# A convolution block of a hybrid decoder: gates for all tokens first, then the values, with one set of weights at a time

## The chip, the cores and the metric

The kernel runs on one core of a Trainium2 chip. The metric is the device time of one execution in microseconds (us), lower is better; a time is the median of the runs shown. A difference of under 0.5% is about what a measurement of this kernel cannot tell from no change.

Engines are named as the profile names them: PE is TensorE (matrix products; PEld is its loading of weights), DVE is VectorE, ACT is ScalarE, POOL is GpSimd, SP is SyncE, which here only issues transfers (DMA). Each engine takes its instructions in order; between engines they wait for each other by semaphores.

## The reference

One layer of a decoder over 2048 prompt tokens and 32 sample tokens (8 sequences of 4). The input is normalised and multiplied by one wide matrix `w_in`, whose columns feed three branches (windowed attention, a gated causal convolution, cross-attention to a memory), their gates, and the merge. What matters here is the second branch:

```
h = _rmsnorm(x, g_pre) @ w_in
qa, ka, va, za, ub, zb, qc, zc, gt = jnp.split(h, SPLITS, axis=-1)
...
glu = ub[..., :EB] * jax.nn.sigmoid(ub[..., EB:])
...
full = jnp.concatenate([hist_conv, glu], axis=1)
conv = lax.conv_general_dilated(full, conv_w[:, None, :], window_strides=(1,), padding='VALID', ...,
                                feature_group_count=EB) + conv_b
```

`EB` is 768, so `ub` has 768 value columns and 768 gate columns; the convolution is 31 wide, one filter per channel.

## The kernel before, in words

The program has three stages, one after the other on PE: projections (`phase_a1`, up to about 898 us of the profiled execution), then the cross-attention, sample attention and windowed attention, with more projections as filler, then the merge and output (`phase_c`). The change lies in the first stage alone.

**Products in three passes.** All products keep float32 precision by splitting each factor into a high part `hi` and a remainder `lo`. `gemm` (line 156) multiplies eight blocks of 128 input channels; for each block it issues `hi` weights by high input (line 162), `hi` weights by low input (163), and `lo` weights by high input (164). The normalised input, as high and low parts for all 2080 tokens, lies in SBUF (tiles `x0h`, `x0l`, `x1h` and so on, the digit being the third of the tokens). Tokens go in six pieces, `CHUNKS`: four of 384, one of 256, one of 288.

**Weights.** `load_w` (141) brings 128 columns of a weight matrix in by a DMA on SP's queue (tile `wraw`, pool `wr`, two buffers), and POOL splits them: `whi` (line 55), then `wlo` (line 56), in the pool `w1` with two buffers each. So at most two sets of weights exist at a time; a third can be split only when PE has finished with the oldest.

**Order of the work.** `phase_a1` first computes two blocks of `q`, then goes through the list `order`: a convolution block `u0`, three plain blocks `k0`, `k1`, `k2`, then `u1`, `k3`, `k4`, `k5`, then `u2`, `v0` to `v2`, `u3`, `v3` to `v5`, `u4`, `q2` to `q4`, `u5`, `q5`, `qc0` to `qc3`. A plain block (`blk_x`, `chunk`) takes one set of weights for six chunks; ACT moves each result out of PSUM (line 233), and for `k` and `v` PE transposes it (250, 252) and DVE copies the rows (254, 258).

**A convolution block** (`blk_u`, 262) takes two sets of weights at once, `wb` for the gates and `wa` for the values. For each chunk it computes the gate product, ACT makes `th = tanh` of it (285), it computes the value product, and DVE writes (th + 1) x value into `G` (290; the sample tokens into `GS`, 295). Before that it clears the margins of `G` on POOL (268; `G` has two buffers) and brings in the old state of the sample sequences (`st_in`, 271, transposed at 275, copied at 277). Results of the products go through PSUM tiles `g`, four buffers.

**The convolution itself** (`conv`) runs on DVE alone: 60 instructions over `acc` and `G` (305, 314) and small ones for the sample tokens (317, 320), then the new state: `so` (325 to 327), three transposes on PE (`trc`, 330, 332), copies to `sr` (334, 335), and transfers on SP (`d_c` at 322, `conv_p` and `conv_s` at 337 and 338). It is issued with a lower priority (`later(LAG)`), so its instructions are spread under the blocks that follow.

**What sets the order on each engine** is a scheduler in the framework: it simulates the program with its own costs and priorities and writes one fixed order per engine. Instructions whose data come late in its simulation are put behind others.

Of the kernel before, what the change touches and what calls it, by code (L numbers as in the profile page):

```python
# [7 lines left out]
F32 = mybir.dt.float32  # L8
R32 = mybir.dt.float32r
AF = mybir.ActivationFunctionType  # L10
# [8 lines left out]
T = S + NS  # L19
HA, DA, EA = 12, 64, 768  # L20
EB, CW = 768, 31
# [9 lines left out]
CHUNKS = [(0, 384), (384, 384), (768, 384), (1152, 384), (1536, 256), (1792, 288)]  # L31
# [3 lines left out]
CQ, CK, CV, CZA, CUB, CZB, CQC, CZC, CGT = 0, 768, 1536, 2304, 3072, 4608, 5376, 5888, 6400  # L35


class K:
# [222 lines left out]

    def blk_u(self, j, wp, stg, cnv, psg, pst):
        nc, I, O = self.nc, self.I, self.O
        wb = self.load_w(wp, self.win(CUB + EB + j * 128), 8, rp=self.wr)
        wa = self.load_w(wp, self.win(CUB + j * 128), 8, rp=self.wr)
        G = cnv.tile([128, 16, 130], F32, name="G", bufs=2)
        GS = cnv.tile([128, 8, 34], F32, name="GS", bufs=2)
        nc.gpsimd.memset(G[:, :, 0:2], 0.0)

        st_in = cnv.tile([120, 2, 128], F32, name="st_in")  # L270
        nc.sync.dma_start(st_in, I["state_conv"][0, :, :, j * 128:(j + 1) * 128]
                          .rearrange("(x b) w c -> x (b w) c", x=2).rearrange("x q c -> q x c"))
        p = pst.tile([128, 512], F32, name="tr")
        for x in range(2):
            nc.tensor.transpose(p[:, x * 128:x * 128 + 120], st_in[:, x, :], self.ident[:120, :120])
        for x in range(2):
            nc.vector.tensor_scalar(GS[:, 4 * x:4 * x + 4, 0:30],
                                    p[:, x * 128:x * 128 + 120].rearrange("p (b w) -> p b w", b=4),
                                    2.0, None, op0=ALU.mult)
        for s, n in CHUNKS:  # L280
            xs = [self.x_at(k, s, n) for k in range(8)]
            pb = psg.tile([128, 512], F32, name="g")
            self.gemm(pb[:, :n], wb, xs)
            th = stg.tile([128, 384], F32, name="th")
            nc.scalar.activation(th[:, :n], pb[:, :n], AF.Tanh, scale=0.5)
            pa = psg.tile([128, 512], F32, name="g")
            self.gemm(pa[:, :n], wa, xs)
            m = min(n, S - s)
            r0 = s // 128
            nc.vector.scalar_tensor_tensor(G[:, r0:r0 + m // 128, 2:130],  # L290
                                           th[:, :m].rearrange("p (r i) -> p r i", i=128), 1.0,
                                           pa[:, :m].rearrange("p (r i) -> p r i", i=128),
                                           op0=ALU.add, op1=ALU.mult)
            if m < n:
                nc.vector.scalar_tensor_tensor(GS[:, :, 30:34],
                                               th[:, m:n].rearrange("p (b t) -> p b t", t=4), 1.0,
                                               pa[:, m:n].rearrange("p (b t) -> p b t", t=4),
                                               op0=ALU.add, op1=ALU.mult)
        return G, GS
# [995 lines left out]
```

## Time and profile before

| | |
|---|---|
| median of 3 runs | 3205.38 us (3191.82 to 3209.69) |
| profiled execution | 3205.15 us, span 3203.4 us |
| PE busy | 3017.2 us, 94% of the span |
| DVE, POOL, ACT busy | 2041.4, 1349.0, 1123.3 us |
| mean granted TensorE clock | 0.974 |

The span runs from the first to the last instruction; 1.75 us of the profiled execution lie around it. A row of a timeline gives the start, the duration, the engine, the line and the operation, the tile written and those read (`g<-x0h,whi`), the shape, and in brackets the idle time of that engine just before, with what ended it. PE's instructions overlap, so their spacing tells more than their durations.

### The profile page before, as it was taken

The page shows a single profiled execution, that of the slowest core. Times are in us where ns is not written, and L with a number is a line of the kernel's source. Part 1 is how long each engine was busy: PE and PEld are TensorE (multiplying, and loading weights), DVE is VectorE, ACT ScalarE, POOL GpSimd, SP SyncE. Part 2 cuts the span into 40 slices and gives each one's busy share as a digit, 9 for nine tenths or more (in the row PEclk, how much of TensorE's full clock was granted, in tenths as well). Part 3 has the DMA queues.
Part 4 walks back from the last instruction along what each step waited for, and adds up shares of the span by engine and source line. Part 5 has one row for each costly group of instructions (what it writes and reads, how often), then busy time and mean ns, then how long its engine had stood idle before and what let it go on. Part 6 is the DMA issues. An engine that isn't in the chain of part 4 may idle for free. (4 is left out here: it accounts for less than half of the span.)

```text
span 3203.4 us, 55580 instructions
## 1 busy us (share of the span) xinstructions
PE 3017.2 (94%) x20705; PEld 2856.5 (89%) x20705; DVE 2041.4 (64%) x3854; ACT 1123.3 (35%) x2835; POOL 1349.0 (42%) x1048
## 2 busy tenths in 40 slices
PE   7999999999988899999999999999898989999998
PEld 6899999999987889998899999999898967787897
DVE  5296786967967944555637666666657557555653
ACT  5110010000122433334437575766565623222221
POOL 0121222221336546444355576577667444233240
PEclk9899999999998999999999999999999999999999
DMA  6332221211254444378554655566655386757561
GB/s 223 107 99 74 80 58 53 57 62 63 73 170 129 158 138 151 109 224 252 157 139 106 159 131 151 129 171 176 161 140 153 104 273 214 228 171 222 158 201 54
DMA packets 532219, 454.67 MB, mean 142 GB/s; under 512 B 118191, under 2 KB 458581, under 8 KB 531137
## 3 DMA queue, kind: packets, MB, share of 16 engines
q1 hardware_dynamic: 357502, 335.36, 35.7%
q10 hardware_dynamic: 169840, 105.02, 11.5%
q0 software_dynamic: 4608, 10.75, 1.1%
q8 instruction: 164, 2.69, 0.4%
q14 instruction: 105, 0.86, 0.1%
HBM read 332.96 MB, written 118.04 MB: 141 GB/s over the span
## 5 line engine op out<-in xcount | busy, mean ns | idle before, releaser
L162 PE MATMUL gg<-x0h,whi 128*128 128x256 f32 (+1 forms) x2560 | 749.6, 293 | 35.5 <-DVE st L240 27.5
L164 PE MATMUL gg<-x0h,wlo 128*128 128x256 f32 (+1 forms) x2560 | 743.0, 290 | 3.3 <-POOL wlo L56 3.3
L163 PE MATMUL gg<-x0l,whi 128*128 128x256 f32 (+1 forms) x2560 | 744.1, 291 | 0.0
L55 POOL TENSOR_SCALAR whi<-wraw 128x1024 fp32r<-128x1024 f32 x162 | 203.1, 1255 | 952.2 <-PE g L163 547.8
L162 PEld LDWEIGHTS gg<-x0h,whi 128*128 128x128 f32 x2560 | 495.6, 194 | 43.3 <-DVE st L240 24.3
L164 PEld LDWEIGHTS gg<-x0h,wlo 128*128 128x128 f32 x2560 | 495.6, 194 | 6.0 <-POOL wlo L56 3.9
L163 PEld LDWEIGHTS gg<-x0l,whi 128*128 128x128 f32 x2560 | 495.6, 194 | 2.0 <-issue 0.3
L314 DVE SCALAR_TENSOR_TENSOR acc<-G,cw,acc 128x1536 f32<-128x1536 f32 (+15 forms) x354 | 460.5, 1334 | 0.0
L56 POOL TENSOR_TENSOR wlo<-wraw,whi 128x1024 fp32r<-128x1024 f32 x162 | 456.1, 2817 | 9.9 <-PE gg L164 0.6
L151 POOL TENSOR_TENSOR clo<-craw,chi 128x768 fp32r<-128x768 f32 (+1 forms) x96 | 172.0, 1793 | 357.2 <-ACT chi L150 344.8
L614 ACT ACTIVATE P<-T,stm 128x128 f32<-128x128 f32 (+1 forms) x576 | 260.7, 455 | 113.2 <-DVE stm L612 76.1
L162 PE MATMUL pg<-ac,chi 128*128 128x512 f32 (+1 forms) x640 | 229.6, 361 | 16.2 <-ACT chi L150 9.0
L612 DVE CUSTOM_DVE_ANT_0 T<-s,bias 128x128 f32<-128x128 f32 (+1 forms) x576 | 191.7, 357 | 77.7 <-PE s L604 43.2
L164 PE MATMUL pg<-ac,clo 128*128 128x512 f32 (+1 forms) x640 | 228.3, 358 | 5.7 <-POOL clo L151 5.5
L163 PE MATMUL pg<-ac,chi 128*128 128x512 f32 (+1 forms) x640 | 228.9, 358 | 2.8 <-DVE ac L1185 2.8
L233 ACT ACTIVATE st<-g 128x384 f32<-128x384 f32 (+1 forms) x132 | 60.2, 460 | 447.3 <-PE g L164 438.3
L164 PE MATMUL g<-x0h,wlo 128*128 128x384 f32 x544 | 187.1, 347 | 22.1 <-POOL wlo L56 22.1
L163 PE MATMUL g<-x0l,whi 128*128 128x384 f32 x544 | 189.5, 348 | 0.0
L162 PE MATMUL g<-x0h,whi 128*128 128x384 f32 x544 | 187.6, 346 | 0.0
L164 PE MATMUL g<-x1h,wlo 128*128 128x384 f32 x544 | 185.8, 341 | 0.0
L163 PE MATMUL g<-x1l,whi 128*128 128x384 f32 x544 | 185.0, 340 | 0.0
L162 PE MATMUL g<-x1h,whi 128*128 128x384 f32 x544 | 182.6, 339 | 2.3 <-ACT x1h L131 2.3
(329 smaller groups left out, 7477.5 us busy)
## 6 DMA issues: line engine op xcount, KB each, us to landing
wraw<-in_w_in ACTq DMA_DIRECT2D x119, 512.0 KB
d_g<-st ACTq DMA_DIRECT2D x168, 128.0 KB
cb<-d_cf SPq DMA_DIRECT2D x72, 256.0 KB
g<-d_g SPq DMA_DIRECT2D x72, 256.0 KB
wraw<-in_w_in SPq DMA_DIRECT2D x35, 512.0 KB
kvc<-in_cache_k_win SPq DMA_DIRECT2D x8, 1536.0 KB
kvc<-in_cache_v_win SPq DMA_DIRECT2D x8, 1536.0 KB
raw<-d_q SPq DMA_DIRECT2D x48, 256.0 KB
```

Source lines behind the costliest of these rows:

```text
L55: nc.gpsimd.tensor_scalar(hi, raw, 1.0, 1.0, op0=ALU.mult, op1=ALU.mult)
L56: nc.gpsimd.tensor_sub(lo, raw, hi.bitcast(F32))
L151: nc.gpsimd.tensor_sub(lo, raw, hi.bitcast(F32))
L162: nc.tensor.matmul(ps, hi[:, k, :], h, start=k == 0, stop=False)
L163: nc.tensor.matmul(ps, hi[:, k, :], l, start=False, stop=False)
L164: nc.tensor.matmul(ps, lo[:, k, :], h, start=False, stop=k == kb - 1)
L233: nc.scalar.activation(st[:, :n], p[:, :n], AF.Copy, scale=sc)
L314: nc.vector.scalar_tensor_tensor(a3[:, lo:hi], G[:, src:src + hi - lo, 2 - m:130 - m], w, a3[:, lo:hi], op0=ALU.mult, op1=ALU.add)
L612: nc.vector.tensor_tensor_reduce(sc[:, :w], t[:, o:o + w], bias[:, 256 - w:256], 1.0, 3.0e38, ALU.add, ALU.min, m)
L614: nc.scalar.activation(P[:, o:o + w], sc[:, :w], AF.Exp, bias=m, scale=-1.0, accum_out=self.stl[:, col:col + 1])
```

## The change

`blk_u` no longer interleaves gates and values. It loads the gate weights, computes all six chunks of gates, and ACT writes their tanh into a new tile `gate` of 2080 columns (one buffer; 8,320 bytes per partition). Then it loads the value weights into a further buffer of the same pools, computes all six chunks of values, and DVE forms `G` and `GS` from `gate` and the products. The tile `th` (three buffers of 384 columns, 4,608 bytes per partition in all) is gone. The clearing of `G` and the fetching of `st_in` now stand ahead of the weights in the code. Nothing else is touched; the number and the shapes of all instructions are the same.

```
     def blk_u(self, j, wp, stg, cnv, psg, pst):
         nc, I, O = self.nc, self.I, self.O
-        wb = self.load_w(wp, self.win(CUB + EB + j * 128), 8, rp=self.wr)
-        wa = self.load_w(wp, self.win(CUB + j * 128), 8, rp=self.wr)
         G = cnv.tile([128, 16, 130], F32, name="G", bufs=2)
...
+
+        w = self.load_w(wp, self.win(CUB + EB + j * 128), 8, rp=self.wr)
+        gate = cnv.tile([128, T], F32, name="gate")
         for s, n in CHUNKS:
-            xs = [self.x_at(k, s, n) for k in range(8)]
             pb = psg.tile([128, 512], F32, name="g")
-            self.gemm(pb[:, :n], wb, xs)
-            th = stg.tile([128, 384], F32, name="th")
-            nc.scalar.activation(th[:, :n], pb[:, :n], AF.Tanh, scale=0.5)
+            self.gemm(pb[:, :n], w, [self.x_at(k, s, n) for k in range(8)])
+            nc.scalar.activation(gate[:, s:s + n], pb[:, :n], AF.Tanh, scale=0.5)
+        w = self.load_w(wp, self.win(CUB + j * 128), 8, rp=self.wr)
+        for s, n in CHUNKS:
+            th = gate[:, s:s + n]
             pa = psg.tile([128, 512], F32, name="g")
-            self.gemm(pa[:, :n], wa, xs)
+            self.gemm(pa[:, :n], w, [self.x_at(k, s, n) for k in range(8)])
             m = min(n, S - s)
             r0 = s // 128
             nc.vector.scalar_tensor_tensor(G[:, r0:r0 + m // 128, 2:130],
```

**PE, block u1, from the end of its first gate chunk.** Before, with buffer numbers (`whi_2242` and `wlo_2243` are the gate weights, `whi_2248` and `wlo_2249` the value weights, `g_2289` the first value chunk, `g_2315` the second gate chunk):

```order
L162 MATMUL g_2289<-x0h0_186,whi_2248 128x384
L163 MATMUL g_2289<-x0l0_194,whi_2248 128x384
L162 MATMUL g_2315<-x0h0_186,whi_2242 128x384
L163 MATMUL g_2315<-x0l0_194,whi_2242 128x384
L164 MATMUL g_2315<-x0h0_186,wlo_2243 128x384
L162 MATMUL g_2315<-x0h1_187,whi_2242 128x384
L163 MATMUL g_2315<-x0l1_195,whi_2242 128x384
L164 MATMUL g_2315<-x0h1_187,wlo_2243 128x384
L162 MATMUL g_2315<-x0h2_188,whi_2242 128x384
L163 MATMUL g_2315<-x0l2_196,whi_2242 128x384
L164 MATMUL g_2315<-x0h2_188,wlo_2243 128x384
L164 MATMUL g_2289<-x0h0_186,wlo_2249 128x384
```

In the program after, at the same place (`whi_2247` and `wlo_2248` are the gate weights, `g_2278` the second gate chunk):

```order
L164 MATMUL g_2252<-x0h7_193,wlo_2248 128x384
L162 MATMUL g_2278<-x0h0_186,whi_2247 128x384
L163 MATMUL g_2278<-x0l0_194,whi_2247 128x384
L164 MATMUL g_2278<-x0h0_186,wlo_2248 128x384
L162 MATMUL g_2278<-x0h1_187,whi_2247 128x384
L163 MATMUL g_2278<-x0l1_195,whi_2247 128x384
L164 MATMUL g_2278<-x0h1_187,wlo_2248 128x384
```

Before, the first `wlo` product of the value weights stood some ten products behind the end of the first gate chunk, with as much of the second gate chunk as the scheduler put in between; now five more gate chunks stand ahead of any product with value weights.

**DVE, block u1, around the end of the convolution of u0** (`acc` is the running sum of that convolution, `G<-...` the products of u1). Before:

```order
L290 SCALAR_TENSOR_TENSOR G<-th,g 128x3x128
L314 SCALAR_TENSOR_TENSOR acc<-G,cw,acc 128x1536
L320 SCALAR_TENSOR_TENSOR acc<-GS,cw,acc 128x32
L314 SCALAR_TENSOR_TENSOR acc<-G,cw,acc 128x384
L314 SCALAR_TENSOR_TENSOR acc<-G,cw,acc 128x1664
L320 SCALAR_TENSOR_TENSOR acc<-GS,cw,acc 128x32
L314 SCALAR_TENSOR_TENSOR acc<-G,cw,acc 128x256
L290 SCALAR_TENSOR_TENSOR G<-th,g 128x3x128
L314 SCALAR_TENSOR_TENSOR acc<-G,cw,acc 128x1792
L320 SCALAR_TENSOR_TENSOR acc<-GS,cw,acc 128x32
L290 SCALAR_TENSOR_TENSOR G<-th,g 128x3x128 x2
L290 SCALAR_TENSOR_TENSOR G<-th,g 128x2x128 x2
```

After:

```order
L322 SCALAR_TENSOR_TENSOR acc<-GS,cw,acc 128x32
L316 SCALAR_TENSOR_TENSOR acc<-G,cw,acc 128x256
L316 SCALAR_TENSOR_TENSOR acc<-G,cw,acc 128x1792
L322 SCALAR_TENSOR_TENSOR acc<-GS,cw,acc 128x32
L292 SCALAR_TENSOR_TENSOR G<-gate,g 128x3x128 x4
L292 SCALAR_TENSOR_TENSOR G<-gate,g 128x2x128 x2
L297 SCALAR_TENSOR_TENSOR GS<-gate,g 128x8x4
L307 TENSOR_SCALAR acc<-G,cw,vecs 128x2048
```

The first two writes of `G` stood inside the tail of the previous convolution; now all six stand behind it, in one row. Line numbers after line 289 are two higher in the program after.

Three more places in words. On POOL the order is that of before: gate weights of u1, value weights of u1, the clearing of the `G` of u2, weights of `k3`. On SP the transfers `d_c` of a convolution and the raw weights keep their places; `conv_p` and `conv_s` stand three to six transfers later, in the middle of the next plain block. The three `trc` transposes on PE moved with them, from the end of u1 into the third chunk of `k3` (behind u2, u3 and u4 into the fourth or fifth chunk of the plain block or earlier, behind u5 into the second plain block), and the copies to `sr` on DVE, which wait for them, stand behind the first eleven or more `acc` instructions over `G` of the next convolution, where they stood ahead of all of them. From the second chunk of `qc0` on, PE's order is the same to the end of the program.

## Rows read from the trace of the kernel before

**Rows 1.** The page: the span, and PE's busy time, share and instructions.

```profile
span 3203.4 us, 55580 instructions
...
PE 3017.2 (94%) x20705; PEld 2856.5 (89%) x20705; DVE 2041.4 (64%) x3854; ACT 1123.3 (35%) x2835; POOL 1349.0 (42%) x1048
```

**Rows 2.** PE's waits from 0 to 1100 us: total, times, longest.

```profile
PE g L164 <- POOL wlo L56: 22.1, 4, 5.6
```

**Rows 3.** Timeline of PE in block u1.

```profile
242.82 0.69 PE L164 MATMUL g<-x0h,wlo 128*128 128x384 f32 x1 [5.58 <-POOL wlo L56]
...
246.02 0.33 PE L162 MATMUL g<-x0h,whi 128*128 128x384 f32 x1
```

**Rows 4.** Stretches: length, busy PE, PEld, DVE, ACT, POOL, granted clock, DMA, GB/s.

```profile
240.00:250.00 10.00, 7.18 (x33) 7.18 (x34) 9.09 (x13) 0.00 (x0) 2.77 (x1) 0.83 0.28 79
...
300.00:320.00 20.00, 20.00 (x135) 19.87 (x134) 20.00 (x23) 2.28 (x5) 4.28 (x2) 1.00 0.36 105
```

**Rows 5.** Timeline of POOL around block u1.

```profile
230.57 3.13 POOL L55 TENSOR_SCALAR whi<-wraw 128x1024 fp32r<-128x1024 f32 x1 [17.81 <-PE g L163]
233.78 8.98 POOL L56 TENSOR_TENSOR wlo<-wraw,whi 128x1024 fp32r<-128x1024 f32 x1
257.77 0.13 POOL L268 MEMSET G<- 128x32 f32 x1 [15.01 <-DVE acc L314]
...
281.93 2.40 POOL L56 TENSOR_TENSOR wlo<-wraw,whi 128x1024 fp32r<-128x1024 f32 x1
```

**Rows 6.** Timeline of ACT: the gates of blocks u1 to u5.

```profile
235.36 0.49 ACT L285 ACTIVATE th<-g 128x384 f32<-128x384 f32 x1 [4.25 <-PE g L164]
250.92 0.49 ACT L285 ACTIVATE th<-g 128x384 f32<-128x384 f32 x1 [15.07 <-PE g L164]
259.31 0.49 ACT L285 ACTIVATE th<-g 128x384 f32<-128x384 f32 x1 [7.89 <-PE g L164]
...
362.84 0.49 ACT L285 ACTIVATE th<-g 128x384 f32<-128x384 f32 x1 [4.25 <-DVE acc L314]
379.40 0.49 ACT L285 ACTIVATE th<-g 128x384 f32<-128x384 f32 x1 [16.07 <-PE g L164]
...
491.32 0.49 ACT L285 ACTIVATE th<-g 128x384 f32<-128x384 f32 x1 [4.25 <-PE g L164]
506.86 0.49 ACT L285 ACTIVATE th<-g 128x384 f32<-128x384 f32 x1 [15.04 <-PE g L164]
...
618.78 0.49 ACT L285 ACTIVATE th<-g 128x384 f32<-128x384 f32 x1 [4.24 <-PE g L164]
635.36 0.49 ACT L285 ACTIVATE th<-g 128x384 f32<-128x384 f32 x1 [16.10 <-PE g L164]
...
741.66 0.49 ACT L285 ACTIVATE th<-g 128x384 f32<-128x384 f32 x1 [3.70 <-PE g L164]
750.40 0.49 ACT L285 ACTIVATE th<-g 128x384 f32<-128x384 f32 x1 [8.26 <-PE g L164]
```

**Rows 7.** Timeline of DVE: the convolution of u0, from its start to its end.

```profile
157.47 1.88 DVE L305 TENSOR_SCALAR acc<-G,cw,vecs 128x2048 f32<-128x2048 f32 x1
...
175.73 2.48 DVE L314 SCALAR_TENSOR_TENSOR acc<-G,cw,acc 128x1280 f32<-128x1280 f32 x2
...
181.77 4.93 DVE L314 SCALAR_TENSOR_TENSOR acc<-G,cw,acc 128x1024 f32<-128x1024 f32 x2
...
255.16 0.56 DVE L290 SCALAR_TENSOR_TENSOR G<-th,g 128x384 f32<-128x384 f32 x1 [1.36 <-PE g L164]
...
257.63 0.25 DVE L320 SCALAR_TENSOR_TENSOR acc<-GS,cw,acc 128x32 f32<-128x32 f32 x1
```

**Rows 8.** PE's waits from 895 to 1000 us, behind the stage of the change.

```profile
PE sco L662 <- DVE sm L660: 9.0, 2, 5.8
PE gg L162 <- DVE st L240: 7.2, 3, 4.6
PE str L654 <- DVE sm L652: 4.7, 3, 1.6
```

## The prediction

> **What bounds the kernel now.** I read the page first: PE is busy for 3017.2 of 3203.4 us, 94% [rows 1]. So only what PE does or waits for counts, and the question is what PE loses in the stage that is changed, up to 898 us. The table of PE's waits answers that: behind the start-up, its one large entry there is a product with low weights that waits for POOL's split, 22.1 us in four waits, the longest 5.6 [rows 2]. The timeline shows where: in u1, PE stands still for 5.58 us ahead of the first product with the value weights' low part, and goes on slowly: that product takes 0.69 us, one of the same size 3.2 us later 0.33 [rows 3]. In that stretch of 10 us the mean granted clock is 0.83, where it is 1.00 in an undisturbed stretch in which PE is busy throughout [rows 4]. So a stall is paid twice, as idle time and as products at the lower of the two levels behind it.
>
> Why the value weights come late is seen on POOL. Two buffers exist; the gate weights of u1 have one, and the other is freed only when k2 ends. POOL starts the value split then, at 230.57, so PE leaves k2 at about 231, and finishes at 233.78 + 8.98 = 242.76 [rows 5]; PE goes on at 242.82 [rows 3]. PE needs these weights one gate chunk after the end of k2, some 4 us, and the split takes 12.2.
>
> **What the change removes.** I price all of it, idle time and slow products, on ACT, which runs the tanh of each gate chunk as soon as PE has it. Between two gate chunks lie one gate and one value chunk, 768 columns; undisturbed that takes 259.31 - 250.92 = 8.39 us. From the first to the second gate chunk of u1 to u5 it takes 15.56, 16.56, 15.54, 16.58 and 8.74 us [rows 6], 72.98 in all, so 72.98 - 5 x 8.39 = 31.0 us more than undisturbed. Of these, 22.1 are the waits, and 8.9 are slow products and small change; u5, which follows plain blocks without rows to copy, loses 0.35 only. u0 follows the start-up and has no such loss.
>
> **Where it goes.** In the new order the value weights are needed one whole set of gates later. Six chunks are 2080 columns, at 8.39 us for 768 columns 22.7 us. The buffer is freed where it was, so they are ready 12.2 us into 22.7, with 10.5 us to spare. So each half of a convolution block becomes what a plain block is today, and plain blocks, with the same two buffers, show no wait.
>
> The next set in line is that of k3. Its buffer is freed when the gates end, at about 231 + 22.7 = 253.7. But on POOL the clearing of the G of u2 stands ahead of it, and that waits for the end of u0's convolution: it ran at 257.77 [rows 5], just as DVE ended at 257.63 + 0.25 [rows 7]. So the split begins at 258 at the latest, takes 12.2 us at the worst seen, and ends by 270; PE needs it when the values end, at 231 + 45.4 = 276.4. The margin is 6 us at the worst. With DVE idle between its writes of G, the low split took 2.40 us instead of 8.98 [rows 5], which would add 6.6 us to the margin. The set behind it, of k4, starts when the values end and has a plain block's time, as today.
>
> **What it adds.** All six writes of G now come within 23 us, behind the tail of the previous convolution on DVE. That convolution ended at 257.9; the first value chunk ends at about 253.7 + 4.2 = 257.9. PE has four buffers for results, so the first must be free only three chunks later, 12.6 us. No cost, with 12.6 us of cover; if the tail came later than that, PE would wait for DVE microsecond for microsecond.
>
> The copies to `sr` now make DVE wait for three transposes on PE that stand in the third chunk of k3, behind 0.61 of its products. Behind them on DVE are the rest of the convolution and the copies of rows to come. DVE gets there after about what lies between 157.47 and 175.73 today [rows 7], 18 us; PE is there after 15, by columns 0.61 x 22.7 = 13.8 plus a few transposes. I take zero; the bound is a few us of DVE time, which the 12.6 us cover. On SP, the transfers of the new state stand behind stores of k3, and nothing reads them in the kernel.
>
> In u0 PE's first products stand in another order beside the bias products; the nearest row is u5's excess of 0.35 us [rows 6], so 0, give or take 1 or 2 us. The tile `gate` moves what the later stages find freed in SBUF; PE's waits there are 9.0, 7.2 and 4.7 us, 20.9 in all, for DVE [rows 8]. The orders there are the same, so I take 0; the bounds are that half of it goes, or that as much again comes, -10 to +21.
>
> **The sum.** 3205.15 us of the profiled execution - 31.0 = 3174.1. The median of the runs is 3205.38, 0.2 us away, so I leave it at 3174.
>
> **A rule against it.** The rows show first that POOL and DVE hinder each other: the low split took 8.98 us beside the convolution and 2.40 beside an idle DVE [rows 5], and in turn two convolution instructions beside another split took 4.93 us where larger ones took 2.48 [rows 7]. The Trainium skill, GPSIMD Engine Reference, "Key points", says why: GpSimd shares its SBUF interfaces with VectorE, and they contend where a DVE instruction has two SBUF inputs, as the convolution's have. By that rule a split put beside more of the convolution lengthens both, and the forecast could turn into the third rival below. The trace agrees on the mechanism, but the number of splits is the same and one of them now meets an almost idle DVE, so I give that rival a small chance.
>
> **The rivals.** First, the gain comes and a part is given back behind the stage. For it: the stage after is tangled, with waits in turn on DVE, ACT and transfers, and the tiles lie elsewhere. Against it: the orders are the same and the convolution of u5 hangs on PE's own progress. At half of the 20.9 us it gives 3174 + 10 = 3184, at all of it 3195.
>
> Second, the change does not do what it says: the wait only moves, from the first value chunk to the first chunk of k3, since POOL must now clear G before it splits for k3. It takes a convolution end more than 6 us later than today. Then each block loses some 5.5 us and its slow products again, and the time is 3205, no change. Against it: the convolution's tail now holds writes of G that wait for PE, 1.36 us for one of them [rows 7], and loses them.
>
> Third, slower than before: DVE's tail decides. If the contention lengthens a convolution so that it ends later than the 12.6 us of cover allow, PE waits for a buffer in each of five blocks (u1 to u5). Slower than before needs 31/5 = 6.2 us beyond the cover, an end 19 us later than today; at 10 us beyond it is 3174 + 5 x 10 = 3224, and with slow products of 2 us each 3234. At the 2.4 us or so that a split cost DVE in the row above, it would take eight more splits a block, and there are five.
>
> **How the numbers follow.** The forecast has a chance of 0.80, the gain partly given back 0.12, the wait that moves 0.05, DVE's tail 0.03. The range goes from 3160, the forecast less some 10 us of the later waits and a few us by which the median of a few runs moves (the runs shown lie from 3191.82 to 3209.69), to 3190, which takes in the first rival up to 16 us. A measurement of this kernel can tell about 0.5%, 16 us, from no change, so faster means under 3189.4: the forecast almost whole and most of the first rival, 0.89; the same 0.08, from the second and the rest; slower 0.03.
>
> **What would show it.** Right: no wait of PE for POOL's low split between 100 and 870 us, first to second gate chunk in u1 to u4 at about 4.2 us (one chunk now), a granted clock of 1.00 in these stretches, and the first product of the next stage some 31 us earlier. Wrong: a wait of PE at the first chunk of k3 behind POOL (second rival), a wait for DVE's writes of G (third), or larger waits in the 100 us after the stage (first).

## The result, and the profile after

The changed kernel takes 3169.14 us, median of the runs (3156.1 to 3174.24); the kernel before takes 3204.91 beside it. The ratio is 0.9888 [0.9869, 0.9906], 35.8 us less. The forecast was 3174, in the range 3160 to 3190. In a second comparison (e9 below) the ratio was 0.9899 [0.988, 0.9919].

The page of after, span and busy engines, as [rows 1]:

```profile
span 3154.0 us, 55551 instructions
...
PE 2992.8 (95%) x20705; PEld 2837.2 (90%) x20705; DVE 2037.6 (65%) x3854; ACT 1123.6 (36%) x2835; POOL 1368.9 (43%) x1048
```

The count of matrix products is the same, PE's busy time is 24.4 us less in this execution and 16.3 us less in that of e9. In the stage of the change, from the start to the mark `st<-gg` that is explained below, the same 5317 products keep PE busy for 851.51 us before and 838.67 after (838.22 in e9):

```profile
0.00:900.87 900.87, 851.51 (x5317) 835.16 (x5318) 644.61 (x838) 124.08 (x259) 198.49 (x80) 0.98 0.27 87
```

```profile
0.00:864.82 864.82, 838.67 (x5317) 825.51 (x5318) 642.36 (x838) 124.31 (x260) 216.06 (x80) 0.99 0.28 90
```

So of the 36.05 us by which this stage is shorter, 12.8 are products that went faster and 23.2 are idle time of PE that is gone.

The table of PE's waits has no row at all between 116 and 860 us, where [rows 2] had 22.1 us behind POOL. The stretch of 240 to 250 us of [rows 4] (length, busy time of PE, PEld, DVE, ACT and POOL, granted clock, DMA, GB/s) reads after:

```profile
240.00:250.00 10.00, 10.00 (x73) 10.00 (x71) 9.84 (x12) 1.29 (x3) 0.27 (x2) 1.00 0.24 68
```

PE is busy throughout and the granted clock stays at 1.00, the upper level, where [rows 4] had 7.18 us of 10 and 0.83.

ACT's timeline of after gives the marks of the stage, as [rows 6]: the first tanh of u0, the first two of u1, the first of u2, and ACT's first instruction on a result of the filler products behind the stage (`st<-gg`), which I use as the stage's end:

```profile
111.64 0.49 ACT L284 ACTIVATE gate<-g 128x384 f32<-128x384 f32 x1 [9.97 <-PE g L164]
...
230.69 0.49 ACT L284 ACTIVATE gate<-g 128x384 f32<-128x384 f32 x1 [4.25 <-DVE acc L316]
234.86 0.49 ACT L284 ACTIVATE gate<-g 128x384 f32<-128x384 f32 x1 [3.67 <-PE g L164]
...
350.90 0.49 ACT L284 ACTIVATE gate<-g 128x384 f32<-128x384 f32 x1 [4.26 <-DVE acc L316]
...
864.82 0.38 ACT L239 ACTIVATE st<-gg 128x256 f32<-128x256 f32 x1 [2.74 <-PE gg L164]
```

The same marks of before, as far as [rows 6] does not have them:

```profile
116.28 0.49 ACT L285 ACTIVATE th<-g 128x384 f32<-128x384 f32 x1 [14.82 <-PE g L164]
...
900.87 0.38 ACT L239 ACTIVATE st<-gg 128x256 f32<-128x256 f32 x1 [2.74 <-PE gg L164]
```

The stage ends 900.87 - 864.82 = 36.05 us earlier. From u1's first tanh to the end it is 665.51 us before and 634.13 after, 31.38 less: what the prediction summed up. The other 4.67 us are won ahead of u1 (235.36 against 230.69), and they are already there at u0's first tanh (116.28 against 111.64). The rest of the program took 3203.4 - 900.87 = 2302.5 us before and 3154.0 - 864.82 = 2289.2 in this execution, the shortest of its six; in e9 the stage ended at 865.14, the span was 3165.0, and the rest 2299.9. So those 13.3 us are mostly spread of the executions: PE is busy 11.6 us less there for the same products (2165.73 against 2154.11). The median's 35.8 us agree with the stage's 36.

POOL's timeline of after at the place of [rows 5]:

```profile
225.90 3.07 POOL L55 TENSOR_SCALAR whi<-wraw 128x1024 fp32r<-128x1024 f32 x1 [17.86 <-PE g L163]
229.05 9.05 POOL L56 TENSOR_TENSOR wlo<-wraw,whi 128x1024 fp32r<-128x1024 f32 x1
249.73 0.13 POOL L266 MEMSET G<- 128x32 f32 x1 [11.63 <-DVE acc L316]
249.84 1.05 POOL L55 TENSOR_SCALAR whi<-wraw 128x1024 fp32r<-128x1024 f32 x1
250.97 2.40 POOL L56 TENSOR_TENSOR wlo<-wraw,whi 128x1024 fp32r<-128x1024 f32 x1
272.05 1.05 POOL L55 TENSOR_SCALAR whi<-wraw 128x1024 fp32r<-128x1024 f32 x1 [18.67 <-PE g L163]
```

The split of the value weights is as slow as before (12.2 us) and ends at 238.10; PE's first value product comes at 249.13, 11 us later. The split for `k3` ends at 253.37, and PE leaves the values when it frees the buffer for the next split, at 272.05: 18.7 us to spare.

DVE's timeline at the end of u0's convolution, as the end of [rows 7]:

```profile
249.60 0.24 DVE L322 SCALAR_TENSOR_TENSOR acc<-GS,cw,acc 128x32 f32<-128x32 f32 x1
253.57 0.56 DVE L292 SCALAR_TENSOR_TENSOR G<-gate,g 128x384 f32<-128x384 f32 x1 [3.73 <-PE g L164]
```

The convolution ends 8 us earlier than before, 3.4 of them against u1's own start, which is 4.7 us earlier itself. DVE then waits for the value chunks, 3.73 us for the first, and not PE for DVE.

### The profile page after: what moved, and what is told of

It reads as the page before. It is cut to its first block, busy times and chain, and to the rows that moved or that the text cites. A ratio compares the mean times of both kernels' runs of the same rounds, so it can differ in the third digit from the quotient of the medians.

```text
span 3154.0 us, 55551 instructions
## 1 busy us (share of the span) xinstructions
PE 2992.8 (95%) x20705; PEld 2837.2 (90%) x20705; DVE 2037.6 (65%) x3854; ACT 1123.6 (36%) x2835; POOL 1368.9 (43%) x1048
## 3 DMA queue, kind: packets, MB, share of 16 engines
q10 hardware_dynamic: 169840, 105.02, 11.6%
q0 software_dynamic: 4608, 10.75, 1.1%
## 5 line engine op out<-in xcount | busy, mean ns | idle before, releaser
L55 POOL TENSOR_SCALAR whi<-wraw 128x1024 fp32r<-128x1024 f32 x162 | 221.4, 1368 | 918.0 <-PE g L163 534.7
```

What stands on the lines that cost most here:

```text
L55: nc.gpsimd.tensor_scalar(hi, raw, 1.0, 1.0, op0=ALU.mult, op1=ALU.mult)
```

## The experiments

Two questions stand. Is the wait for the second set of weights all that u1 to u5 had to lose (and what covers it now)? And what won 4.7 us in u0, which the prediction had at nothing? The theory for the second came from reading the two traces beside each other around u0's start, PE's timeline of before:

```profile
99.33 2.10 PE L354 MATMUL tr<-oh,rb 33*12 33x384 f32 x6
101.36 0.44 PE L162 MATMUL g<-x0h,whi 128*128 128x384 f32 x1
101.64 0.34 PE L163 MATMUL g<-x0l,whi 128*128 128x384 f32 x1
101.90 0.92 PE L364 MATMUL tr<-ohs,rb 33*12 33x376 f32 x2
102.75 0.69 PE L162 MATMUL g<-x0h,whi 128*128 128x384 f32 x1
...
104.97 3.93 PE L364 MATMUL tr<-ohs,rb 33*12 33x376 f32 x6
```

and of after:

```profile
99.36 2.10 PE L356 MATMUL tr<-oh,rb 33*12 33x384 f32 x6
101.39 0.44 PE L162 MATMUL g<-x0h,whi 128*128 128x384 f32 x1
...
103.00 2.06 PE L366 MATMUL tr<-ohs,rb 33*12 33x376 f32 x6
104.99 0.45 PE L164 MATMUL g<-x0h,wlo 128*128 128x384 f32 x1
105.27 0.34 PE L162 MATMUL g<-x0h,whi 128*128 128x384 f32 x1
```

The bias products (`bias_rows`: 33 rows of weights, 12 columns; a row of the trace counts each twice) lie between the token products of u0. Before, one `ohs` product came two token products behind the three `oh` ones, and from then on token products took longer, 0.69 us and then 0.52; after, eight token products lie between, and they go on at 0.34. The stretch 103 to 105 us, before and then after, with the granted clock in the third place from the end:

```profile
103.00:105.00 2.00, 2.00 (x7) 1.56 (x8) 0.39 (x1) 0.00 (x0) 2.00 (x2) 0.50 0.63 200
```

```profile
103.00:105.00 2.00, 2.00 (x8) 0.47 (x7) 1.07 (x2) 0.00 (x0) 2.00 (x2) 1.00 0.63 197
```

The clock is 0.50, the lower level, from 103 to 111 us before, and 1.00 after. Nothing in PE's waits shows it, for PE is busy all the time in both. The whole fall in the kernel before lies in this stretch:

```profile
102.00:113.00 11.00, 11.00 (x28) 6.63 (x28) 2.89 (x6) 0.00 (x0) 3.96 (x3) 0.53 0.53 165
```

With the clock at 0.53 in the mean, PE can do in these 11 us at most 5.2 us less work than at 1.00; that is an estimate, and it lies near the 4.7 us.

Marks in us from ACT's timeline: first tanh of u0 and u1, from u1's first tanh to u2's and to the first `st<-gg`, the time of that, and what is left of the profiled execution's span.

| | u0 | u1 | u1 to u2 | u1 to st<-gg | st<-gg | rest | ratio to before |
|---|---|---|---|---|---|---|---|
| before | 116.28 | 235.36 | 127.48 | 665.51 | 900.87 | 2302.5 | |
| after | 111.64 | 230.69 | 120.21 | 634.13 | 864.82 | 2289.2 | 0.9888 [0.9869, 0.9906] |
| e1, u0 old | 116.10 | 235.20 | 120.21 | 634.13 | 869.33 | 2300.8 | 0.9896 [0.9874, 0.9918] |
| e2, u0 alone new | 111.12 | 230.18 | 128.80 | 666.18 | 896.36 | 2299.4 | 0.9981 [0.9962, 0.9999] |
| e3, third set | 115.95 | 240.09 | 121.16 | 639.28 | 879.37 | 2279.4 | 0.9875 [0.9856, 0.9894] |
| e4, before, bias later | 108.17 | 235.20 | 127.45 | 665.44 | 900.64 | 2285.5 | 0.9944 [0.9924, 0.9964] |
| e5, after, bias later | 123.48 | 234.52 | 120.21 | 634.13 | 868.65 | 2277.8 | 0.9845 [0.9811, 0.988] |
| e6, split twice | 112.98 | 232.01 | 120.20 | 634.15 | 866.16 | 2309.0 | 0.9901 [0.9869, 0.9933] |
| e7, conv + 12 us | 113.10 | 232.15 | 120.22 | 634.42 | 866.57 | 2312.0 | 0.9897 [0.9859, 0.9935] |
| e8, conv + 30 us | 113.19 | 232.25 | 126.12 | 744.29 | 976.54 | 2301.3 | 1.0215 [1.0184, 1.0247] |
| e9, after again | 111.96 | 231.01 | 120.21 | 634.13 | 865.14 | 2299.9 | 0.9899 [0.988, 0.9919] |
| e10, e5 again | 125.01 | 234.86 | 120.20 | 634.13 | 868.99 | 2277.5 | 0.9859 [0.9841, 0.9878] |

In e5 and e10 ACT makes the first four tanh of u0 in one row, behind the last bias products; their mark of u0 can't be set beside the others, that of u1 can.

### e1 and e2: the change in u0 apart from u1 to u5

Both kernels have the two forms of the block, the old one with `th` as a slice of `gate`:

```
+    def blk_u_old(self, j, wp, stg, cnv, psg, pst):
...
-                        gs = self.blk_u(j, wp, stg, cnv, psg, pst)
+                        gs = (self.blk_u if j > 0 else self.blk_u_old)(j, wp, stg, cnv, psg, pst)
```

e2 has `j == 0` in that place.

> The changed kernel with one convolution block of six, u0, written in the old way (gates and values in turn, both sets of weights at once); u1 to u5 are as changed. PE's order around the bias products (tr<-oh, tr<-ohs) is again that of the kernel before, with one ohs product two token products behind the oh ones. Theory of the clock: the 4.7 us that the changed kernel won ahead of u1 hang on that order, so the granted clock falls to 0.50 again behind the ohs products, u1's first tanh comes at about 235.4 us (before 235.36, after 230.69) and the first filler result of stage one's end (st<-gg) at 900.9 - 31.4 = 869.5 us. Rival, chance: the fall in the kernel before was of that one execution and can be absent here; then about 230.7 and 864.8. Both expect the spacing u1 to u2 at 120.2 us, since it is the waits of u1 to u5 alone that the 31 us come from. Ratio to before 0.990 to 0.992 (clock) or 0.988 to 0.990 (chance).

> The other half: u0 alone is written in the new way, u1 to u5 are as before. The order around the bias products is that of the changed kernel. Theory of the clock: no fall of the clock at 100 to 113 us, u1's first tanh at about 230.7 us, the spacing u1 to u2 127.5 us as before, the four waits for wlo (22.1 us) back, the first st<-gg at 900.9 - 4.7 = 896.2 us, ratio 0.998 to 0.999. Rival, chance: the clock may fall here too, and u1's first tanh then comes at 235.4 us, st<-gg at 900.9. Rival, gains are not additive (the whole new order is needed): the waits of u1 to u5 change in size though their code is the old.

Both came out as the theory of the clock has it, the marks of u1 and of the end to 0.5 us (e2's u1 to u2 is 1.3 us longer than forecast; of that 0.7 us are left at the end of the stage). In e1 the order around the bias products is that of before, and the clock falls (103 to 105 us):

```profile
103.00:105.00 2.00, 2.00 (x7) 1.30 (x6) 0.06 (x1) 0.00 (x0) 2.00 (x2) 0.50 0.58 174
```

In e2 it is that of after, and the clock is 1.00 in that stretch, while the waits of u1 to u5 are back in full:

```profile
PE g L164 <- POOL wlo L56: 22.1, 4, 5.5
```

The two parts add up: e1's stage is 31.54 us shorter than before, e2's 4.51, together 36.05. As times of the whole program they are 0.9896 and 0.9981; the second is at the edge of what the runs can tell, so it is the marks that carry it.

### e3: a third set of weights, gates and values still in turn

```
-        wa = self.load_w(wp, self.win(CUB + j * 128), 8, rp=self.wr)
+        wa = self.load_w(cnv, self.win(CUB + j * 128), 8, rp=self.wr, split=('vhi', 'vlo'))
...
-        hi = pool.tile([128, kb, n], R32, name=tag + "hi")
-        lo = pool.tile([128, kb, n], R32, name=tag + "lo")
+        hi, lo = (pool.tile([128, kb, n], R32, name=x)
+                  for x in split or (tag + "hi", tag + "lo"))
...
-            th = stg.tile([128, 384], F32, name="th")
+            th = stg.tile([128, 384], F32, name="th", bufs=2)
```

Room is made by `th` alone; the kernel that ran has as many `xt` tiles as the one before.

> The kernel before, gates and values in turn, but the split value weights of a convolution block have buffers of their own (vhi, vlo, 8 KB per partition), so that three sets can exist; room is made with five instead of six tiles of input rows (xt) and two instead of three of th. Theory of the waits: all that the change won in u1 to u5 is the wait for the second set and the products that a lower clock slows behind it, so here too the waits for wlo go, the spacing u1 to u2 is 120.2 us instead of 127.5, and four to five blocks win 31 us without gates being put ahead of values. Rival, it is the new order itself that helps (a long run of products with one set, tanh and G apart): the spacing stays at 127.5 us or falls by less than half. Fewer xt tiles may cost some us ahead of 100 us; the first block of u tells that apart.

The waits for the low split are gone, and u1 to `st<-gg` falls from 665.51 to 639.28: 26.2 us of the 31.4 without putting gates ahead of values. What is left is another wait (240 to 880 us, all of PE's):

```profile
PE tr L275 <- DVE ro L254: 3.9, 2, 1.9
PE tr L250 <- ACT st L233: 0.7, 1, 0.7
```

The transposes of `st_in` now stand where they need a PSUM tile that DVE has yet to empty. So most of the gain of u1 to u5 is that of a set of weights that is there in time, however it is brought about; the 5.1 us that e3 lacks go with this other wait, which the new order does not have. The u0 of e3 shows the fall of the clock too, here with a wait of 1.34 us in it:

```profile
102.88 3.93 PE L364 MATMUL tr<-ohs,rb 33*12 33x376 f32 x6 [1.34 <-DVE ext L355]
```

Ahead of u1 e3 loses more than the kernel before: u1's first tanh is at 240.09, 4.7 us later. PE waits there once more, 2.16 us for `st_in`, and behind that wait the clock falls a second time (0.50 from 123 to 125 us).

The time of the whole is as good as that of the changed kernel (0.9875), though its stage ends 14.6 us later (9.4 of them ahead of u1): the rest of its program is shorter. I come back to that under e5.

### e4, e5: the bias products elsewhere

Both times, in the kernel before (e4) and in the changed one (e5):

```
-                self.bias_rows(self.cpool, bp, pst)
+                with self.later(LAG):
+                    self.bias_rows(self.cpool, bp, pst)
```

> The kernel before with nothing but the bias rows (oh, ohs and their small products) issued with a lower priority, so that three oh products stand eight token products behind u0's start and the ohs products come later still. Theory of the clock: without an ohs product closely behind the oh ones the granted clock does not fall, products stay at 0.33 to 0.35 us, u1's first tanh comes 4.7 us earlier than before, at about 230.7 us, and st<-gg at about 896 us. Rival, chance: the place of the bias products does not decide, the clock falls in some executions and not in others, or falls here as well at 0.50 for about 9 us. Rival, form of u0: the 4.7 us come from the new form of u0, not from the clock, and stay at 235.4 us here.

> The changed kernel with the bias rows issued at a lower priority: now one ohs product follows directly on the three oh products, and the other five come together some 90 token products later. Theory of the clock (small bias products that lie close together let the granted clock fall): the fall to 0.50 that the changed kernel did not have is back, once behind the five or already behind the first four, and u1's first tanh comes 4 to 9 us later than in the changed kernel (230.69), at 235 to 240 us, the first st<-gg at 869 to 874 us; u1 to u5 keep the spacing 120.2 us. Rival, the new form of u0 is what won 4.7 us: 230.7 and 864.8 us. Ratio to before 0.988 to 0.992.

e4 was half a miss. u0's first tanh came at 108.17, and the clock stayed at 1.00 from 97 to 115 us, but u1's came at 235.20, as before. The six `ohs` products now stand in one row later in u0, and the fall came behind them instead (PE's timeline of e4):

```profile
132.18 3.96 PE L365 MATMUL tr<-ohs,rb 33*12 33x376 f32 x12
137.32 0.66 PE L162 MATMUL g<-x1h,whi 128*128 128x384 f32 x1 [1.18 <-DVE G L291]
```

So it is not the form of u0 (e4 has the old one and no fall at 103, e5 the new one and a fall), and not chance either. e5 shows both cases in one run: three `oh` products and one `ohs` product in a row, 2.7 us, after which the token products go on at full speed, and later five in a row, after which they are slow:

```profile
101.86 2.10 PE L357 MATMUL tr<-oh,rb 33*12 33x384 f32 x6
103.80 0.79 PE L367 MATMUL tr<-ohs,rb 33*12 33x376 f32 x2
104.53 0.44 PE L164 MATMUL g<-x0h,wlo 128*128 128x384 f32 x1
...
120.10 3.35 PE L367 MATMUL tr<-ohs,rb 33*12 33x376 f32 x10
124.03 0.58 PE L162 MATMUL g<-x2h,whi 128*128 128x256 f32 x1 [0.58 <-ACT gate L285]
124.40 0.42 PE L163 MATMUL g<-x2l,whi 128*128 128x256 f32 x1
```

The wait of 0.58 us is not what brought the clock down: the granted clock falls already while PE is busy with the last of the five.

```profile
123.20:123.40 0.20, 0.20 (x1) 0.00 (x0) 0.17 (x1) 0.00 (x0) 0.00 (x0) 0.71 0.00 0
```

It cost 3.8 us: `st<-gg` at 868.65 against 864.82, a little less than the 869 to 874 expected.

Yet the times of both fell: e4 by 0.56% against before with the same end of the stage, e5 below the changed kernel. Their rest is shorter (2285.5 and 2277.8 us, against 2289 to 2312 in all others but e3 and e10, which is e5 again). Profiled executions scatter; with the median span of each kernel's runs in place of the profiled one (an estimate, since the mark is from one execution) the rest is 2282 to 2285 us in e3, e4, e5 and e10, and 2297 to 2307 in all others, 2302 both before and after. That is not the stage's doing. With the lower priority of the bias rows the scheduler writes another order for the later stages, as it does in e3, and PE waits less in them: it is idle for 119 to 123 us of the rest in these four, for 135 to 145 us in the others. Which of the many moves does it was not tried, so the cause stays open.

### e6: how much time the split has

```
-            self.split_pool(hi, lo, raw)
+            for _ in range(2 if twice else 1):
+                self.split_pool(hi, lo, raw)
```

with `twice` for the value weights alone.

> The changed kernel with the split of each block's value weights made twice on POOL, the second time over the first (same numbers). In u1 this puts the end of the split from 238.1 to about 250 us, and the first product that needs it comes at about 253 us. Theory of the cover (the second set has a whole run of six gate chunks to be made ready): no wait for wlo comes back in u1 to u3, the spacing u1 to u2 stays at 120.2 us and the ratio at 0.988; in u4 and u5, where whi alone took 7 and 20 us in the changed kernel, up to 10 us in all may show. Rival, the margin is thinner than that and POOL's queue behind it (the clearing of G, k3's split) is what counts: a wait of 3 to 12 us in each of u1 to u5, 15 to 60 us in all, the ratio at 0.993 to 1.007.

No wait for a split came back in any block, and from u1's first tanh to the end of the stage it takes what the changed kernel takes to 0.02 us. The second split of u1 cost 5.2 us and not 12, and ended at 244.78, 5.7 us ahead of PE's first value product at 250.45. It does not show where the cover ends, only that it is more than this. (The 20 us that the expectation gives to u5 belong to a plain block behind it, as told at the end.)

### e7, e8: how much time DVE's tail has

```
+        junk = cnv.tile([128, 6, 128], F32, name="junk")
...
+        for x in range(12):
+            nc.vector.scalar_tensor_tensor(junk, a3[:, 0:6], self.cw[:, j, 0:1], G[:, 0:6, 2:130],
+                                           op0=ALU.mult, op1=ALU.add)
```

and 30 instead of 12 in e8. As they ran in a block, the twelve kept DVE busy for 14.2 us and the thirty for 35.0.

> The changed kernel with twelve more instructions of 128x768 in each convolution on DVE (their result goes to a tile nobody reads), 1.00 us each by the rows of the changed kernel, so 12 us a block. DVE is busy 100.6 us of the 120.2 between u1 and u2. Theory of the cover: 3.7 us of DVE's idle time ahead of the first write of G and three value chunks of 4.2 us in the four PSUM tiles (12.6 us) hide it; the spacing stays at 120.2 us, the first st<-gg at 864.8 to 870 us, ratio 0.988 to 0.990. Rival (the prediction's third: the tail of the convolution delays the writes of G): PE waits for PSUM tiles that DVE has not emptied, up to 12 us a block, 60 us in all, ratio up to 1.007.

> The same with thirty more instructions, 30 us a block: DVE would be busy 130.6 us in a block of 120.2. Theory of the cover: 16.3 us are hidden and then the tail reaches PE; DVE is the bound, the spacing u1 to u2 becomes 130 us or some us more, PE waits for DVE's writes of G or copies of rows, some 50 us in the stage, and the convolution of u5 ends later, which may delay the filler products and the normalisation behind it by up to 30 us more; ratio 1.004 to 1.014. Rival, DVE has room that the rows don't show (the convolution is spread under the plain blocks too): less than 20 us in all, ratio under 0.995.

e7: no cost, as the cover has it. DVE is busy 114.93 of the 120.2 us of a block, and its first write of `G` in u1 comes late, behind seven of the added instructions (DVE's timeline; the changed kernel has it at 253.57, and e7 runs 1.5 us later there):

```profile
252.05 9.36 DVE L320 SCALAR_TENSOR_TENSOR junk<-acc,cw,G 128x768 f32<-128x768 f32 x7
261.32 0.55 DVE L292 SCALAR_TENSOR_TENSOR G<-gate,g 128x384 f32<-128x384 f32 x1
```

e8 was a miss in both halves. DVE is the bound, but the blocks lost less than expected: 126.12, 121.37, 128.96 and 116.71 us from tanh to tanh against 120.21, 120.19, 120.24 and 114.55, 18 us in all, where some 10 us in each were expected. And I had the end of it too small: the convolutions have fallen behind, and behind u5's PE runs out of work, which costs 92 us more. PE's waits of e8 from 232 to 1000 us, the three longest, all behind u5, and the two of the blocks that tell what PE waits for there:

```profile
PE sco L668 <- DVE sm L666: 33.9, 2, 26.6
PE tr L917 <- DVE mt L913: 29.5, 1, 29.5
PE gg L162 <- DVE st L240: 11.2, 1, 11.2
PE tr L273 <- DVE ro L254: 9.6, 2, 5.1
...
PE g L162 <- DVE G L292: 1.7, 2, 1.2
```

From u1's first tanh to `st<-gg` it takes 110 us more than in the changed kernel, and the ratio is 1.0215, above the expected 1.004 to 1.014. So DVE as the bound is a real danger, and the changed kernel is between twelve and thirty such instructions per block away from it. But the wait that the prediction's third rival names, for a buffer that DVE's writes of `G` free too late, is only 1.7 us of it; in the blocks PE waits mostly for DVE's copies of rows.

### e9, e10: the changed kernel and e5 side by side

The kernels are those of after and of e5.

> The changed kernel once more, beside the next one on the same chip. By the runs so far its ratio to before is 0.9888 [0.9869, 0.9906]. If the marks of stage one are fixed by the order of the program and not by chance, u1's first tanh minus u0's is 119.05 us (119.06 in the kernel before, 119.05 in the changed one), the spacing u1 to u2 120.2 us and first st<-gg minus u1's first tanh 634.1 us, with the granted clock at 1.00 from 100 to 115 us. Under the rival (the fall of the clock is chance) the clock may fall here.

> The kernel of e5 once more, in more rounds beside the changed kernel. In e5 stage one ended 3.8 us later than in the changed kernel, yet the time was 0.9845 [0.981, 0.988] of before. If that is real (the order of the later stages that comes out with the bias rows at a lower priority is better by some 10 to 18 us, as it was in e4 against the kernel before at 0.9944) the ratio is again 0.983 to 0.986, 8 to 18 us under the changed kernel's; if it was spread of the runs, the two are within 5 us of each other or this one is 4 us slower.

The marks of e9 repeat to 0.3 us, with the clock at 1.00 from 97 to 145 us. By now six profiled executions have this order around the bias products (after, e2, e6 to e9) and none shows the fall; those of before and e1, with the old order, and of e5 and e10, with the third, all do. So the order decides, not chance. e10 is 3155.98 us against e9's 3170.11, 14 us less, with its stage ending 3.9 us later; so by the medians its rest is some 18 us shorter (22 in the profiled executions). It is the best kernel of this study, by an order of the later stages that came out of the scheduler and that nobody chose.

## Why the prediction was right, and where a term was off

- **The gain of 31.0 us** (waits of 22.1 and slow products of 8.9): measured 31.38 from u1 to the end of the stage, 31.4 in e1. First to second gate chunk is 4.17 us in u1 where about 4.2 was forecast. e3 and e2 show it from both sides: a set in time without the new order wins most of it (26.2), u0 alone in the new order none.
- **10.5 us to spare for the value split:** 11 us in u1. **6 us at the worst for `k3`:** 18.7, since the convolution ended earlier, 3.4 us against u1's start, and the split met an idle DVE (1.05 and 2.40 us, as [rows 5] had for 2.40) where 12.2 us were reckoned. The second rival, a wait that moves there, is out.
- **Six writes of `G` behind the convolution's tail, no cost with 12.6 us of cover:** none, and none in e7 with 14 us more; the third rival is out at this size of the convolution. The copies to `sr` came at 291.54 with no wait.
- **u0 at 0, give or take 1 or 2 us** is the term that was mis-sized: it measured -4.7 us. I took u5's excess of [rows 6] as the nearest row, wrote of u0 that it "has no such loss", and did not look at the clock where PE is busy. The row that would have told was in the trace of before, 0.50 from 103 to 111 us, and the order of PE showed that the bias products would stand apart. e1, e2, e4 and e5 show that their place decides.
- **Later stages at 0 (-10 to +21):** 2302.5 us before and 2299.9 in e9; 2289.2 in the profiled execution of after, 2302 by the median of its runs. The waits just behind the stage (860 to 970 us) are 9.1, 8.8 and 4.7 us, 22.6 against the 20.9 of [rows 8]. The first rival, a gain given back there, is not to be seen.
- **The sum:** 31.4 and 4.7 make 36, the median's 35.8. The 3169 measured lie 5 us under the 3174 forecast, about what the term of u0 lacks; the other terms came out as they were summed, so no errors cancelled.
- **The Trainium skill's rule** (GPSIMD Engine Reference, "Key points") on SBUF interfaces that GpSimd shares with VectorE had its mechanism here (9.05 us for the low split beside the convolution, 2.40 beside an idle DVE) and did not cost PE anything; how close one split came is told below.

## What to carry to other kernels

Where two sets of weights are used in turn, the second must be ready one chunk after the first; if the sets are used one after the other, the whole run of the first hides the loading of the second, and no memory for a third set is needed (here the third set won 26 of 31 us, the order all of it). Count the clock where PE is busy as well as where it waits: a few small products lying together cost 4 to 5 us here with no idle time and no row in the table of waits. And ask of every engine that is not the bound how far it is from being it: DVE could take 14 us more in a block for nothing, and 35 us more cost 110 in the stage and behind it.

## What the runs showed that I had not expected

**The clock falls under a busy PE.** In six of the profiled kernels (before, e1, e3, e4, e5, e10) the granted clock went down in u0, to 0.50 where the stretch read is short enough to show it, behind bias products of 33 rows and 12 columns. Ahead of the fall stood three `oh` products, two token products and one `ohs` product (before, e1), or three `oh` products, two token products and a wait of 1.34 us, in whose course it fell (e3), or six or five `ohs` products in a row (e4, e5, and e10, whose order is that of e5; it fell between 0.1 us ahead of their end and 0.9 us behind it). Three in a row between token products (after, 2.06 us), or four (e5, 2.7 us), did not. PE was busy throughout in before and e1. Why these products let it fall is not shown; that their place decides is. The Trainium skill, TensorE: Matmul & The Clock Gate, "HAM oscillation — how this bites in real kernels", speaks of gaps in which PE is idle; here a PE that the profile calls busy lost its clock as well.

**POOL can be shut out by DVE almost completely.** In the changed kernel, at the end of u5's convolution, where DVE has no rows to copy, one split took 19.83 us where 1.05 is its best:

```profile
815.95 19.83 POOL L55 TENSOR_SCALAR whi<-wraw 128x1024 fp32r<-128x1024 f32 x1 [16.76 <-PE g L163]
835.86 2.39 POOL L56 TENSOR_TENSOR wlo<-wraw,whi 128x1024 fp32r<-128x1024 f32 x1
```

The last instruction of that convolution on DVE, after 20 us of instructions without a gap:

```profile
834.76 1.04 DVE L322 SCALAR_TENSOR_TENSOR acc<-GS,cw,acc 128x32 f32<-128x32 f32 x1
```

The split ends at 835.78, inside that instruction, which takes 1.04 us where others of its size take 0.23; so POOL got in there and DVE waited for it in turn. The low part follows and ends at 838.25, and PE begins the next block at 838.62: 0.4 us were left. It was not the end of the convolution that let POOL in, for in e7 DVE goes on for 17 us behind that instruction, and the split took 19.86 us all the same. The Trainium skill, SBUF — State Buffer, "SBUF: two separate sides", says that the pair of ports the two share is an exclusive lock and that the other one blocks. The rows agree, as far as POOL's spans can be read that closely; that DVE had it time after time for 19 us, over some two dozen of its instructions with two tiles as input, is what they add. It came with the change: after, e1, e5, e6, e7, e9 and e10 all have this split at 19.80 to 19.86 us, while before, e2, e3 and e4 have no high part over 7.8 us in this stage. What decides that POOL gets in is open.
